# One 512-column pass for both parts of the operand, into two halves of a PSUM bank, with groups of two column tiles

## The chip, the cores and the metric

The kernel runs on one core of a Trainium2 chip. The metric is the device time of one execution in microseconds (us); lower is better. Engines are named as in the profile: PE is TensorE (matmul), PEld its weight load, DVE is VectorE, ACT ScalarE, POOL GpSimd, SP the sync engine, whose queue issues nearly all DMAs.

## The reference

Two layers act on a stream `h` of 256 positions by 4096 features; both also attend to a fixed memory of 256 tokens. All data are float32.

```
for i in range(2):
    proj = rmsnorm(h, pre_norm[i]) @ w_in[i]          # 4096 -> u 3072 | gate 3072 | q 1024 | q_gate 1024
    u, gate, q, q_gate = split(proj)
    y = s5_mixer(u) if i == 0 else rglru_mixer(u)
    kv = rmsnorm(mem, mem_norm[i]) @ w_kv[i]          # 4096 -> 2048
    m = 4-head softmax attention of q into kv
    out = concat([y * silu(gate), m * silu(q_gate)]) @ w_out[i]   # 4096 -> 4096
    h = h + rmsnorm(out, post_norm[i])
```

The S5 mixer is a complex diagonal state-space scan over the 256 positions (192 groups of 16 channels, 64 states each), then GELU and a gate by a product with a 3072 x 3072 matrix (`glu`). The RG-LRU mixer is a short convolution, two block-diagonal gates and a first-order recurrence.

## The kernel before, in words

**Products.** A float32 weight tile W and operand tile X are each split into a high and a low part of type float32r: `hi`, `lo` and `X[:, 0]`, `X[:, 1]`. Of the four products three are kept: `hi` by X high, `hi` by X low, `lo` by X high. Weights are the stationary side (128 x 128), the operand moves with its 256 positions, and the result is one column tile of 128 features by 256 positions in PSUM. In the V projections alone (`vproj`) the operand is stationary and 512 columns of weights move. The operand of a layer lies in SBUF as `[128, 2, 32, 256]`: part, row tile, position.

**The weight stream.** `add_phase` (L268) makes a list of 980 steps; each step takes one chunk of 512 KB, which is 8 weight tiles: usually 2 row tiles by 4 column tiles (`mc=4, kc=2`). A group of four column tiles needs 16 steps over 32 row tiles; it holds two PSUM banks, two column tiles in each. The phases in order are u0 (96 steps), g0 (96), gq0, q0, k0, v0, k1 (32 each), glu (72), out0 (128), v1 (32), u1 (96, with 12 gate steps of the RG-LRU between them and the phases after), gq1, q1 (32 each), g1 (96) and out1 (128). The first 8 tiles of u0 come in chunks of 8 x 1, the next 4 in chunks of 2 x 4.

**One turn.** `run` (L367) goes turn by turn, and what it emits is the program order of all engines. In a turn it first runs what is due (`at(k, f)` puts f into turn k) and the hooks of that step, then `mm_step(i)`, 24 matmuls, then `split_w(i + 2)`: two ScalarE casts of 512 columns to `hi`, and VectorE subtractions to `lo` that wait in a list `pieces`. Then comes `run_side`, the rest of the pieces, and `load_w`, the weight DMA some steps ahead (three buffers `raw`, six halves each of `hi` and `lo`). A turn in which `ready()` of the step is false runs all this without matmuls, and the step waits for the next turn.

**The side work** is generators (S5, attention, set-up of the RG-LRU). `run_side` (L356) takes the next piece of one only while the planner's running estimates allow it:

```
while self.side and self.dve_t < self.pe_t and self.act_t < self.pe_t:
```

The estimates are sums of prices in the code: a matmul of 256 columns 109, one of 512 columns 217, a VectorE tensor operation 1.04 per element and 70 more (`tt`, L74).

**S5** (L674). Its scan runs over 127 times t in two blocks of 48 state pairs. One t is a multiplication `m` (192 elements) and two additions (96 each); between them `seqfill` (L954) takes a waiting piece of the weight split or books 130, and small operations book 20 (`pen`) where no piece is there. In the scan a piece is 256 columns. After a block, `S = self.step + 6`, and `y_tasks(blk, ct, S + 5 * c // 2)` (L840) puts the output of each of 12 channel tiles into fixed turns: load of u at S, product `y_mm` at S + 2, activation steps at S + 3 to S + 8, stores of `gF` and `gHL` at S + 9. Coefficients are made on GpSimd (`y_coef`, L799). The second block's inputs are taken only as the first block's output products are done. `load_g` (L1233) brings the stored `gHL` into the operand buffer A in the turn after it is stored, and the GLU's step kg of the first group is ready once tiles 2 kg and 2 kg + 1 are asked for.

**Operands** are made by `prep_phase` (L252), 16 units of two row tiles, one per turn: two ScalarE and two VectorE operations each, and squares where a row scale is wanted. It starts at k0 - 14 for the memory of k0 and at k1 - 14 for k1, in the buffer A that the product before still reads.

**Evacuation.** When a group ends, its column tiles are evacuated one a turn from PSUM (`ev_*`, L401 to L557): a multiplication by the row scale, then what the phase needs. The output products (`whole`) take the two banks one after the other (`ev_out`, L452).

Of the kernel before, what the change touches and what calls it, by code (L numbers as in the profile page):

```python
# [20 lines left out]
T = 256  # L21
E = 3072
# [18 lines left out]

def size(ap):
    n = 1
    for s in ap.shape[1:]:
        n *= s
    return n


class Trunk:
# [185 lines left out]
    def prep(self, src, gain, layer, dst, ks, square=False, last=False, rb=None, col=None):  # L235
        """Operand tiles ks (a pair) of a normalised matrix: gain applied, split into two float32r parts."""
# [15 lines left out]
    def prep_phase(self, start, src, gain, layer, dst, square=False, rb=None, col=None, spacing=1):  # L252
        """16 units; the one for tiles 2c, 2c+1 runs at step start + c * spacing."""
        def load(c):
            if c >= KD // 2:
                return
            f = self.prep(src, gain, layer, dst(), (2 * c, 2 * c + 1), square, c == KD // 2 - 1, rb, col)

            def go():
                f()  # L260
                load(c + 2)
            self.hook(start + int(c * spacing), go)
        self.hook(start - 3, lambda: load(0))
        self.hook(start - 2, lambda: load(1))

# [1 line left out]
    def add_phase(self, w, nm, ks, operand, evac, mc=4, kc=2, vproj=False, ready=lambda kg: True, m0=0,  # L267
                  whole=False):  # L268
        """Matrix product with weight chunks of kc x mc tiles; ks: operand tiles in order of use."""
        nkg = len(ks) // kc  # L270
        for mg in range(nm // mc):
            grp = {}
            for kg in range(nkg):
                self.steps.append(dict(w=w, idx=mg * nkg + kg, mg=mg, kg=kg, nkg=nkg, grp=grp, mc=mc, kc=kc,
                                       ks=ks[kg * kc:kg * kc + kc], operand=operand, evac=evac, v=vproj, m0=m0, whole=whole,
                                       ready=(lambda mg=mg, kg=kg: mg > 0 or ready(kg))))
# [29 lines left out]
    def mm_step(self, i):  # L306
# [6 lines left out]
        grp, mc, kc = s["grp"], s["mc"], s["kc"]  # L313
        if s["kg"] == 0:
            if s["v"]:
                grp["acc"] = [self.ps_acc.tile([128, 512], F32, name="acc", tag="acc") for _ in range(2)]
            else:
# [3 lines left out]
        if end and not s["v"]:  # L321
            order = [(kk, (m,)) for m in range(mc) for kk in range(kc)]
        for kk, ms in order:
# [4 lines left out]
            if s["v"]:  # L328
                wh, wl = hi[kk], lo[kk]
                for n in range(2):  # L330
                    a = grp["acc"][n]
# [4 lines left out]
            else:  # L336
                for m in ms:
                    a = grp["acc"][m // 2][:, m % 2, :]
                    h, c = (kk * mc + m) // 4, (kk * mc + m) % 4 * 128
                    wh, wl = hi[h][:, c:c + 128], lo[h][:, c:c + 128]  # L340
# [3 lines left out]
        if s["kg"] == s["nkg"] - 1:  # L344
            acc = grp["acc"]
            if s["v"]:
                for n in range(2):
                    self.at(self.step + 1 + 2 * n, lambda n=n: s["evac"](s["m0"] + s["mg"], n, acc[n]))
            else:
                if s["whole"]:  # L350
                    self.at(self.step + 1, lambda: s["evac"](s["mg"] * mc, acc, 0))
                for m in range(0 if s["whole"] else mc):
                    self.at(self.step + 1 + (max(0, m - 1) if mc != 4 else m), lambda m=m: s["evac"](s["m0"] + s["mg"] * mc + m, acc[m // 2][:, m % 2, :]))
        del s["hi"], s["lo"]
# [12 lines left out]
    def run(self):  # L367
        """One turn per weight chunk; a turn without a chunk where its operand is not there yet."""
# [32 lines left out]
    def ev_u0(self, m, ps):  # L401
        """The even times first, then the odd ones."""
# [49 lines left out]
    def ev_out(self, layer, m, accs, i, out, last):  # L452
        """Tiles m, m + 1 of an output product: gain, sum of squares; then those of the next bank."""
# [6 lines left out]
        def b():  # L460
# [4 lines left out]
            if i == 0:  # L465
                self.ev_out(layer, m + 2, accs, 1, out, last)
# [17 lines left out]
    def boundary_begin(self):  # L484
        """h1 = x + out * rstd * gain, then the operand of layer 1; the first loads run ahead."""
# [106 lines left out]
    def exp_gen(self, y, x, t):  # L592
        """y = exp(x); t: list of 5 scratch tiles (the last one int32)."""
# [168 lines left out]
        # -- inputs of the odd states: B u[2t+1] + a B u[2t], two units of 32 channels in the rows --  # L762
# [21 lines left out]
        # -- outputs of the 128 channels ct --  # L784
# [140 lines left out]
    def s5_a_b(self, region, t0, n):  # L925
        """Stages that put a B of n channel tiles, with the channels in the rows, to memory."""
# [34 lines left out]
    def attention(self, layer, X):  # L961
# [21 lines left out]
        for h in range(4):  # L983
# [24 lines left out]
            pT = ap.tile([128, 2, T], F32, name="pT", tag="pT", bufs=1)  # L1008
# [25 lines left out]
    def lru_setup(self):  # L1034
# [8 lines left out]
        # log1p(z) = 2 atanh(z / (2 + z))  # L1043
# [20 lines left out]
    def lru_block(self, b, G):  # L1064
        """Conv, gates (their products in step G) and recurrence of the block's 256 channels."""
# [98 lines left out]
    def build(self):  # L1164
# [8 lines left out]
        allk = list(range(KD))  # L1173
# [4 lines left out]
        self.add_phase(I["w_u0a"], 8, allk, A, self.ev_u0, mc=8, kc=1)  # L1178
        self.add_phase(I["w_u0b"], 4, allk, A, self.ev_u0, mc=2, kc=4, m0=8)
        self.add_phase(I["w_u0c"], KE - 12, allk, A, self.ev_u0, m0=12)  # L1180
        self.add_phase(I["w_g0"], KE, allk, A, self.ev_silu(self.sil))
        self.add_phase(I["w_gq0"], KX, allk, A, self.ev_silu(self.sq[0]))
        self.add_phase(I["w_q0"], KX, allk, A, lambda m, ps: self.ev_row(self.qd[0], self.rbx)(m, ps))
        mark["k0"] = len(self.steps)
        self.add_phase(I["w_k0"], KX, allk, A, self.ev_row(self.kd[0], self.rbm))
        self.add_phase(I["w_v0"], KX, allk, A, self.ev_v(self.vd[0]), vproj=True)
        mark["k1"] = len(self.steps)
        self.add_phase(I["w_k1"], KX, allk, A, self.ev_row(self.kd[1], self.rbm))
        mark["glu"] = len(self.steps)

        self.add_phase(I["w_glu"], KE, list(range(KE)), A, self.ev_glu,
# [3 lines left out]
        self.add_phase(I["w_out0"], KD, list(range(KE, KD)) + list(range(KE)), B, self.ev_out0, whole=True,  # L1195
                       ready=lambda kg: ("att", 0) in self.done)
        mark["v1"] = len(self.steps)
        self.add_phase(I["w_v1"], KX, allk, A, self.ev_v(self.vd[1], "st"), vproj=True)
# [3 lines left out]
        def ev_u1(m, ps):  # L1202
            """One tile a turn, in order, once the row scale is there."""
# [9 lines left out]
        self.add_phase(I["w_u1"], KE, allk, B, ev_u1)  # L1213
        self.add_phase(I["w_gq1"], KX, allk, B, self.ev_silu(self.sq[1]))
        self.add_phase(I["w_q1"], KX, allk, B, lambda m, ps: self.ev_row(self.qd[1], self.rbx)(m, ps))
        mark["gate1"] = len(self.steps)
        self.add_phase(I["w_g1"], KE, allk, B, self.ev_g1)
# [6 lines left out]
        self.add_phase(I["w_out1"], KD, list(range(KE, KD)) + list(range(KE)), A, self.ev_out1, whole=True,  # L1224
                       ready=lambda kg: ("att", 1) in self.done)
# [21 lines left out]
        for k in range(KE):  # L1247
            self.hook(mark["glu"] - 16 + k // 2 + 2, lambda k=k: try_g(k))
# [22 lines left out]
        # the table of the square root is loaded ahead of the chain that needs it  # L1271
# [22 lines left out]
def layout(i):  # L1294
    """Host-side data layout only."""
# [3 lines left out]
    r["mem"] = np.ascontiguousarray(A["mem"][0].T).reshape(KD, 128, T)  # L1299
    for l in range(2):  # L1300
        w = A["w_in"][l]
        if l == 0:
            r["w_u0a"] = lay(w[:, :1024], 8, 1)
            r["w_u0b"] = lay(w[:, 1024:1536], 2, 4)
            r["w_u0c"] = lay(w[:, 1536:E])
        else:
            r["w_u1"] = lay(w[:, :E])
        r[f"w_g{l}"] = lay(w[:, E:2 * E])
        r[f"w_q{l}"] = lay(w[:, 2 * E:2 * E + XA])
        r[f"w_gq{l}"] = lay(w[:, 2 * E + XA:])  # L1310
        kv = A["w_kv"][l]
        r[f"w_k{l}"] = lay(kv[:, :XA])
        r[f"w_v{l}"] = lay(kv[:, XA:])
        o = A["w_out"][l]
        r[f"w_out{l}"] = lay(np.concatenate([o[E:], o[:E]], axis=0))
    r["w_glu"] = lay(A["s5_w_glu"][0])
# [51 lines left out]
```

## Time and profile before

| what | value |
|---|---|
| median of 3 runs | 3026.53 us (3025.53 to 3026.67) |
| span of the profiled execution, first to last instruction | 3025.3 us (its own time is not given apart) |
| PE busy | 2954.0 us, 98% |
| DVE busy | 2024.8 us, 67% |
| ACT busy | 1549.5 us, 51% |
| DMA | 645 MB, mean 213 GB/s |

The span leaves out what lies around the program. Busy times count a pipelined matmul from start to its modelled end, so overlapping passes are counted once as a union: a busy PE says that it always had a pass in flight, not how fast passes follow each other. That is read from the starts in a timeline, or from counts in a window (a count takes in passes that overlap an edge of it).

### The profile page before, as it was taken

To read this page: it belongs to the slowest core of one execution; us is meant where nothing else is said; L and a number is where in the kernel's file an instruction comes from. 1 tells how busy PE (TensorE), PEld (TensorE's weight loads), DVE (VectorE), ACT (ScalarE), POOL (GpSimd) and SP (SyncE) were. 2 spreads that over 40 slices of the span, in tenths; PEclk is the share of its full clock that TensorE was granted. 3 is DMA by queue.
4 is the path that set the end of the run, shared out by engine and by line. 5 is a ranking of instruction groups with operands and counts; after the bars stand their busy time and mean duration, and the time that the engine had idled before them with its cause. 6 is when DMAs were issued, how large, how long until landed. Compare 5 with 4: busy or idle time off the path is not lost.

```text
span 3025.3 us, 64511 instructions
## 1 busy us (share of the span) xinstructions
PE 2954.0 (98%) x24558; PEld 2901.3 (96%) x24558; DVE 2024.8 (67%) x4349; ACT 1549.5 (51%) x2871; POOL 164.0 (5%) x225
## 2 busy tenths in 40 slices
PE   9999999999999999999999998999999999999996
PEld 9999999999998988999999977999999999999996
DVE  8638998559999654656545565677787765645445
ACT  6444444554645644546544444456665655444443
POOL 1000000520000530000000011000000000000001
PEclk9999999999999999999999999999999999999998
DMA  8776656766767787567656588666666665556554
GB/s 266 224 211 213 210 192 204 231 218 201 240 207 229 252 267 241 197 218 241 211 192 198 190 254 238 199 198 216 193 223 205 209 222 184 189 200 197 196 190 159
DMA packets 286391, 644.87 MB, mean 213 GB/s; under 512 B 38912, under 2 KB 158976, under 8 KB 285824
## 3 DMA queue, kind: packets, MB, share of 16 engines
q1 hardware_dynamic: 279872, 634.72, 65.2%
q0 software_dynamic: 4352, 4.20, 0.9%
q8 instruction: 192, 3.15, 0.4%
q10 hardware_dynamic: 1856, 1.84, 0.2%
q14 instruction: 119, 0.97, 0.1%
HBM read 592.81 MB, written 47.81 MB: 212 GB/s over the span
## 4 chain that ended last, share of the span: by engine, by line
PE 89%; DMA 5%; DVE 2%; issue 1%; ACT 1%; SPq 1%; DVEq 0%; ACTq 0%; POOLq 0%
PE acc L116 85%; PE psx L116 1%; PE pm L116 1%; PE psg L116 1%; DMA bh<-in_x 1%; DVE lo L76 1%; SPq L120 1%; DMA u<-uF 1%; DMA st<-in_mem 1%; DMA bo<-og 0%; ACT hi L112 0%; DVE Bfin L76 0%; PE pso L116 0%; PE pss L116 0%; DMA gHL<-gh 0%
## 5 line engine op out<-in xcount | busy, mean ns | idle before, releaser
L76 DVE TENSOR_TENSOR lo<-raw,hi 128x512 fp32r<-128x512 f32 (+1 forms) x2386 | 1355.2, 598 | 864.5 <-ACT hi L112 806.6
L112 ACT CAST hi<-raw 128x512 fp32r<-128x512 f32 x1960 | 1165.1, 619 | 1013.1 <-PE acc L116 718.3
L116 PE MATMUL acc<-A,hi 128*128 128x256 f32 x8320 | 1513.0, 284 | 10.7 <-ACT A L108 6.3
L116 PEld LDWEIGHTS acc<-A,hi 128*128 128x128 f32 x8320 | 1299.7, 192 | 16.5 <-ACT A L108 6.3
L116 PE MATMUL acc<-A,lo 128*128 128x256 f32 x4160 | 1179.6, 284 | 2.3 <-DVE lo L76 2.2
L116 PEld LDWEIGHTS acc<-A,lo 128*128 128x128 f32 x4160 | 799.4, 192 | 4.6 <-DVE lo L76 4.5
L116 PE MATMUL acc<-Bhn,hi 128*128 128x256 f32 x4096 | 742.0, 284 | 7.2 <-ACT hi L112 7.2
L116 PEld LDWEIGHTS acc<-Bhn,hi 128*128 128x128 f32 x4096 | 640.4, 192 | 8.3 <-ACT hi L112 7.8
L116 PE MATMUL acc<-Bhn,lo 128*128 128x256 f32 x2048 | 580.4, 283 | 0.7 <-DVE lo L76 0.7
L116 PEld LDWEIGHTS acc<-Bhn,lo 128*128 128x128 f32 x2048 | 393.6, 192 | 1.3 <-DVE lo L76 1.3
L116 PE MATMUL acc<-Bmix,hi 128*128 128x256 f32 x2048 | 368.7, 283 | 0.0
L116 PEld LDWEIGHTS acc<-Bmix,hi 128*128 128x128 f32 x2048 | 319.5, 192 | 0.0
L116 PE MATMUL acc<-Bmix,lo 128*128 128x256 f32 x1024 | 289.8, 283 | 0.0
L116 PEld LDWEIGHTS acc<-Bmix,lo 128*128 128x128 f32 x1024 | 196.6, 192 | 0.0
L76 DVE TENSOR_TENSOR Bs<-Bs,m 128x96 f32<-128x96 f32 x508 | 169.0, 333 | 4.3
L116 PE MATMUL acc<-hi,A 128*128 128x512 f32 x512 | 160.7, 396 | 11.2 <-ACT hi L112 11.2
L116 PEld LDWEIGHTS acc<-hi,A 128*128 128x128 f32 x512 | 97.0, 191 | 32.9 <-ACT hi L112 12.9
L116 PE MATMUL acc<-lo,A 128*128 128x512 f32 x256 | 101.3, 396 | 0.0
L76 DVE TENSOR_TENSOR m<-A,Bs 128x192 f32<-128x192 f32 x254 | 90.6, 357 | 10.5 <-ACT Bs L112 4.4
L807 POOL TENSOR_TENSOR Bs<-Bs,cf 128x256 f32<-128x256 f32 x48 | 33.3, 693 | 784.6 <-DMA Bs<-in_s5c 418.7
L575 POOL TENSOR_TENSOR Bfin<-Bfin 128x1024 f32<-128x1024 f32 x4 | 10.3, 2586 | 1145.6 <-DVE Bfin L76 1145.6
L108 ACT ACTIVATE e<-e 128x256 f32<-128x256 f32 x64 | 26.8, 418 | 86.8 <-DVE e L76 86.4
(143 smaller groups left out, 1503.9 us busy)
## 6 DMA issues: line engine op xcount, KB each, us to landing
raw<-in_w_out SPq DMA_DIRECT2D x256, 512.0 KB, 3.9
raw<-in_w_g SPq DMA_DIRECT2D x192, 512.0 KB, 3.6
raw<-in_w_u SPq DMA_DIRECT2D x96, 512.0 KB, 3.9
raw<-in_w_glu SPq DMA_DIRECT2D x72, 512.0 KB, 3.8
raw<-in_w_gq SPq DMA_DIRECT2D x64, 512.0 KB, 4.2
raw<-in_w_q SPq DMA_DIRECT2D x64, 512.0 KB, 3.6
raw<-in_w_k SPq DMA_DIRECT2D x64, 512.0 KB, 4.0
raw<-in_w_v SPq DMA_DIRECT2D x64, 512.0 KB, 4.0
```

The source lines that it names most:

```text
L76: self.nc.vector.tensor_tensor(out=out, in0=a, in1=b, op=op)
L108: self.nc.scalar.activation(out=out, in_=a, func=f, **kw)
L112: self.nc.scalar.copy(out=out, in_=a)
L116: self.nc.tensor.matmul(out, lhsT=lhsT, rhs=rhs, start=start, stop=stop)
L120: self.nc.sync.dma_start(out=out, in_=in_)
L575: self.nc.gpsimd.tensor_tensor(out=o, in0=o, in1=h, op=ALU.add)
L807: g.tensor_tensor(out=P, in0=s["craw"], in1=b(re), op=ALU.mult)
```

## The change

Each group of column tiles gets a form: chunks of 8 x 1 (`n8`), 2 x 4 (`n2`), 4 x 2 (`n4`) column by row tiles as before, `v` for the V projections, and a new one, `w2`: 2 column by 4 row tiles. In `w2` each column tile has a bank of its own. One matmul of 512 columns multiplies `hi` by both parts of X, high part into the first half of the bank and low part into the second; one of 256 columns adds `lo` by X high to the second half. At evacuation ScalarE copies the second half into a new SBUF buffer `e0`, VectorE adds the first half, and the old evacuation goes on from SBUF.

Most phases are `w2` throughout. The first 12 tiles of u0, the first 4 of k0, k1 and glu, and the first 8 of u1 keep the old forms. The planner's prices in `w2` are 211 and 105 per pair of tiles. Some loads start later, because a group's last pass over the operand now takes 8 steps and not 16: the operand of k0 at k0 - 6, and the GLU's `gHL` at glu - 8 with four tiles a turn. To make room, `e3` has two buffers instead of three, and `pT` of the attention lies in `p`.

```diff
+SHAPE = {"n8": (8, 1), "n2": (2, 4), "n4": (4, 2), "w2": (2, 4), "v": (4, 2)}
+def blocks(nm, form=None, n=0):
+    return ([(0, n, form)] if form else []) + [(n, nm - n, "w2")]
+FORMS = {"u0": [(0, 8, "n8"), (8, 4, "n2"), (12, KE - 12, "w2")], "g0": blocks(KE), "gq0": blocks(KX), "q0": blocks(KX),
+         "k0": blocks(KX, "n4", 4), "v0": [(0, KX, "v")], "k1": blocks(KX, "n4", 4),
+         "glu": blocks(KE, "n4", 4), "out0": blocks(KD), "v1": [(0, KX, "v")],
+         "u1": blocks(KE, "n4", 8), "gq1": blocks(KX), "q1": blocks(KX), "g1": blocks(KE), "out1": blocks(KD)}
...
-                grp["acc"] = [self.ps_acc.tile([128, 2, T], F32, name="acc", tag="acc") for _ in range(mc // 2)]
+            n = 2 if form == "v" else mc if wide else mc // 2
+            grp["acc"] = [self.ps_acc.tile([128, 2, T], F32, name="acc", tag="acc") for _ in range(n)]
...
-                    a = grp["acc"][m // 2][:, m % 2, :]
+                if wide:
+                    a = acc[m]
+                    self.mm(a, wh, X[:, :, k, :], first, False, 211)
+                    self.mm(a[:, 1, :], wl, xh, False, last, 105)
+                else:
+                    a = acc[m // 2][:, m % 2, :]
                     self.mm(a, wh, xh, first and m % 2 == 0, False, 109)
                     self.mm(a, wh, xl, False, False, 109)
                     self.mm(a, wl, xh, False, last and m % 2 == 1, 109)
...
+    def evacuate(self, s, acc):
...
+        elif s["form"] == "w2":
+            t = self.ev.tile([128, 2, T], F32, name="e0", tag="e0", bufs=1)
+            for m in range(mc):
+                self.at(self.step + 1 + (0 if s["whole"] else 2 * m), lambda m=m: self.acopy(t[:, m, :], acc[m][:, 1, :]))
+            def add(m):
+                self.add(t[:, m, :], t[:, m, :], acc[m][:, 0, :])
+            def both():
+                add(0)
+                add(1)
+                evac(m0, [t], 0)
+            def one(m):
+                add(m)
+                evac(m0 + m, t[:, m, :])
+            if s["whole"]:
+                self.at(self.step + 2, both)
             else:
+                for m in range(mc):
+                    self.at(self.step + 2 + 2 * m, lambda m=m: one(m))
...
-            g, sg, o = self.e("e1"), self.e("e2"), self.e("e3")
+            g, sg = self.e("e1"), self.e("e2")
+            o = self.ev.tile([128, T], F32, name="e3", tag="e3", bufs=2)
...
-            if i == 0:
-                self.ev_out(layer, m + 2, accs, 1, out, last)
+            if i + 1 < len(accs):
+                self.ev_out(layer, m + 2, accs, i + 1, out, last)
...
-            pT = ap.tile([128, 2, T], F32, name="pT", tag="pT", bufs=1)
+            pT = p
...
-        self.prep_phase(mark["k0"] - 14, I["mem"], "memg", 0, A, True, self.rbm, self.colm)
+        self.prep_phase(mark["k0"] - 6, I["mem"], "memg", 0, A, True, self.rbm, self.colm)
...
-            self.hook(mark["glu"] - 16 + k // 2 + 2, lambda k=k: try_g(k))
+            self.hook(mark["glu"] - 8 + k // 4 + 2, lambda k=k: try_g(k))
```

The rest of the diff lays out the weight chunks by the same table and removes comments.

## Rows read from the trace of the kernel before

**Rows 1.** The page, part 1: engine, busy us, share, instructions.

```profile
PE 2954.0 (98%) x24558; PEld 2901.3 (96%) x24558; DVE 2024.8 (67%) x4349; ACT 1549.5 (51%) x2871; POOL 164.0 (5%) x225
```

**Rows 2.** Windows of PE on `acc`: stretch, length, busy, count, clock, DMA share, GB/s.

```profile
920.00:990.00 70.00, 70.00 (x311) 1.00 0.75 242
1500.00:1700.00 200.00, 200.00 (x1670) 1.00 0.60 196
```

**Rows 3.** Timeline of PE at 300 and 925 us: start, us, engine, line, operation.

```profile
300.18 0.28 PE L116 MATMUL acc<-A,lo 128*128 128x256 f32 x1
...
300.54 0.28 PE L116 MATMUL acc<-A,lo 128*128 128x256 f32 x1
...
924.92 0.39 PE L116 MATMUL acc<-lo,A 128*128 128x512 f32 x1
...
925.60 0.39 PE L116 MATMUL acc<-lo,A 128*128 128x512 f32 x1
```

**Rows 4.** Tile view of `m`: count, duration ns min/median/max, first and last start.

```profile
L76 DVE TENSOR_TENSOR m<-A,Bs x254: 342/358/372, 234.2 to 992.6; 128x192 f32<-128x192 f32 x127
```

**Rows 5.** Windows of all engines: PE, PEld, DVE, ACT, POOL, clock, DMA.

```profile
233.50:513.50 280.00, 280.00 (x2336) 280.00 (x2335) 261.69 (x823) 125.38 (x214) 0.00 (x0) 1.00 0.64 202
...
1004.00:1124.00 120.00, 110.60 (x1309) 105.94 (x1308) 68.36 (x112) 64.09 (x160) 62.45 (x96) 0.99 0.81 260
```

**Rows 6.** Chain that ended last, in order of time: start, us, what.

```profile
171.92 1.78 PE psx L116 x16
...
1095.68 1.60 PE pm L116 x50
...
1100.81 3.67 DMA u<-uF
...
1150.77 4.74 DMA gHL<-gh
```

**Rows 7.** Groups of instructions, passes with `lo`: busy us, mean ns, idle before.

```profile
L116 PE MATMUL acc<-A,lo 128*128 128x256 f32 x4160 | 1179.6, 284 | 2.3 <-DVE lo L76 2.2
...
L116 PE MATMUL acc<-Bhn,lo 128*128 128x256 f32 x2048 | 580.4, 283 | 0.7 <-DVE lo L76 0.7
...
L116 PE MATMUL acc<-Bmix,lo 128*128 128x256 f32 x1024 | 289.8, 283 | 0.0
```

**Rows 8.** Groups: a VectorE read of 256 PSUM columns, a ScalarE copy of them.

```profile
L76 DVE TENSOR_TENSOR e<-acc,rbx 128x256 f32<-128x256 f32 x128 | 52.9, 415 | 26.3 <-DMA uF<-e 18.5 <-DMA qd<-e 5.4 <-PE acc L116 2.3
...
L112 ACT COPY Bs<-psa 128x256 f32<-128x256 f32 x1 | 0.4, 374 | 2.6 <-PE psa L747 2.6
```

**Rows 9.** Windows of PE on `acc`, each from the start of the span.

```profile
0.00:538.00 538.00, 507.33 (x4160) 1.00 0.70 218
...
0.00:1124.20 1124.20, 1050.80 (x8272) 1.00 0.71 224
...
0.00:233.50 233.50, 204.69 (x1642) 1.00 0.76 235
...
0.00:660.00 660.00, 613.11 (x5021) 1.00 0.70 220
```

**Rows 10.** Tile views of `psx` and `pm`: passes that read a buffer named `acc`.

```profile
L116 PE MATMUL psx<-acc,W x192: 270/275/275, 542.4 to 660.2; 128*128 128x128 f32 x192
...
L116 PE MATMUL pm<-ones,acc x40: 164/250/271, 75.8 to 3000.9; 128*128 128x1 f32 x40
```

**Rows 11.** Tile views of `Bs`, `gHL` and `u`: GpSimd coefficients, SP issues, DMA landing.

```profile
L807 POOL TENSOR_TENSOR Bs<-Bs,cf x48: 612/616/1089, 523.9 to 1107.3; 128x256 f32<-128x256 f32 x48
...
L809 POOL TENSOR_TENSOR Bs<-Bs,cQ x48: 455/514/967, 525.7 to 1108.6; 128x128 f32<-128x128 f32 x48
...
L120 SPq DMA_DIRECT2D A<-gHL x48: 319/407/1241, 1064.0 to 1156.3; - x48
...
DMA to landing us min/median/max: 3.2/3.8/5.8
```

More of the change, by code (lines that the diff above doesn't have):

```diff
@@ L264, in prep_phase, with add_phase @@
         self.hook(start - 2, lambda: load(1))
[L267 to L276, printed above, removed]
+    def add_phase(self, name, operand, evac, ks=None, whole=False, ready=lambda kg: True):
+        idx = 0
+        first = True
+        w = self.I["w_" + name]
+        for m0, nm, form in FORMS[name]:
+            mc, kc = SHAPE[form]
+            kk = ks or list(range(KD))
+            nkg = len(kk) // kc
+            for mg in range(nm // mc):
+                grp = {}
+                for kg in range(nkg):
+                    self.steps.append(dict(w=w, idx=idx, m=m0 + mg * mc, kg=kg, nkg=nkg, grp=grp, mc=mc, kc=kc,
+                                           ks=kk[kg * kc:kg * kc + kc], operand=operand, evac=evac, form=form,
+                                           whole=whole,
+                                           ready=(lambda kg=kg: ready(kg)) if first else (lambda: True)))
+                    idx += 1
+                first = False
     def load_w(self, i):
@@ L312, in mm_step @@
         X = s["operand"]()
-        grp, mc, kc = s["grp"], s["mc"], s["kc"]
+        grp, mc, kc, form = s["grp"], s["mc"], s["kc"], s["form"]
+        wide = form == "w2"
         if s["kg"] == 0:
-            if s["v"]:
-                grp["acc"] = [self.ps_acc.tile([128, 512], F32, name="acc", tag="acc") for _ in range(2)]
-            else:
-                grp["acc"] = [self.ps_acc.tile([128, 2, T], F32, name="acc", tag="acc") for _ in range(mc // 2)]
+            n = 2 if form == "v" else mc if wide else mc // 2
+            grp["acc"] = [self.ps_acc.tile([128, 2, T], F32, name="acc", tag="acc") for _ in range(n)]
+        acc = grp["acc"]
         end = s["kg"] == s["nkg"] - 1
         order = [(kk, range(mc)) for kk in range(kc)]
-        if end and not s["v"]:
+        if end and form != "v":
             order = [(kk, (m,)) for m in range(mc) for kk in range(kc)]
@@ L327, in mm_step @@
             xh, xl = X[:, 0, k, :], X[:, 1, k, :]
-            if s["v"]:
+            if form == "v":
                 wh, wl = hi[kk], lo[kk]
                 for n in range(2):
-                    a = grp["acc"][n]
+                    a = acc[n].rearrange("p a b -> p (a b)")
                     r = slice(n * 128, n * 128 + 128)
@@ L343, in mm_step @@
                     self.mm(a, wl, xh, False, last and m % 2 == 1, 109)
[L344 to L348, printed above, removed]
-            else:
[L350 to L354, printed above, removed]
+        if end:
+            self.evacuate(s, acc)
+        del s["hi"], s["lo"]
+    def evacuate(self, s, acc):
+        m0, mc, evac = s["m"], s["mc"], s["evac"]
+        if s["form"] == "v":
+            for n in range(2):
+                self.at(self.step + 1 + 2 * n, lambda n=n: evac(m0 // 4, n, acc[n].rearrange("p a b -> p (a b)")))
+        elif s["form"] == "w2":
[13 more added lines that the diff above has]
+                self.at(self.step + 2, both)
+            else:
+                for m in range(mc):
+                    self.at(self.step + 2 + 2 * m, lambda m=m: one(m))
+        elif s["whole"]:
+            self.at(self.step + 1, lambda: evac(m0, acc, 0))
+        else:
+            for m in range(mc):
+                self.at(self.step + 1 + (max(0, m - 1) if mc != 4 else m),
+                        lambda m=m: evac(m0 + m, acc[m // 2][:, m % 2, :]))
     def run_side(self):
@@ L1172, in build @@
         self.A = self.big.tile([128, 2, KD, T], F32R, name="A", tag="A")
-        allk = list(range(KD))
         A, B = (lambda: self.A), (lambda: self.B)
@@ L1176, in build @@
         mark = {}
[L1178 to L1183, printed above, removed]
+        self.add_phase("u0", A, self.ev_u0)
+        self.add_phase("g0", A, self.ev_silu(self.sil))
+        self.add_phase("gq0", A, self.ev_silu(self.sq[0]))
+        self.add_phase("q0", A, lambda m, ps: self.ev_row(self.qd[0], self.rbx)(m, ps))
         mark["k0"] = len(self.steps)
[L1185 to L1186 removed]
+        self.add_phase("k0", A, self.ev_row(self.kd[0], self.rbm))
+        self.add_phase("v0", A, self.ev_v(self.vd[0]))
         mark["k1"] = len(self.steps)
[L1188 removed]
+        self.add_phase("k1", A, self.ev_row(self.kd[1], self.rbm))
         mark["glu"] = len(self.steps)
[L1191 removed]
+        self.add_phase("glu", A, self.ev_glu, ks=list(range(KE)),
                        ready=lambda kg: ("gload", 2 * kg + 1) in self.done)
         mark["out0"] = len(self.steps)
[L1195 removed]
+        self.add_phase("out0", B, self.ev_out0, ks=list(range(KE, KD)) + list(range(KE)), whole=True,
                        ready=lambda kg: ("att", 0) in self.done)
         mark["v1"] = len(self.steps)
[L1198 removed]
+        self.add_phase("v1", A, self.ev_v(self.vd[1], "st"))
         mark["u1"] = len(self.steps)
@@ L1299, in layout @@
     r["mem"] = np.ascontiguousarray(A["mem"][0].T).reshape(KD, 128, T)
+    W = {"glu": A["s5_w_glu"][0]}
     for l in range(2):
[L1301 to L1316, printed above, removed]
+        w, kv, o = A["w_in"][l], A["w_kv"][l], A["w_out"][l]
+        W[f"u{l}"], W[f"g{l}"] = w[:, :E], w[:, E:2 * E]
+        W[f"q{l}"], W[f"gq{l}"] = w[:, 2 * E:2 * E + XA], w[:, 2 * E + XA:]
+        W[f"k{l}"], W[f"v{l}"] = kv[:, :XA], kv[:, XA:]
+        W[f"out{l}"] = np.concatenate([o[E:], o[:E]], axis=0)
+    for n, w in W.items():
+        r["w_" + n] = np.concatenate([lay(w[:, m * 128:(m + c) * 128], *SHAPE[f]) for m, c, f in FORMS[n]])
     ga = np.stack([A["lru_w_a"][0], A["lru_w_x"][0]], axis=1)
```

18 lines of the change are left out of this document (9 added, 9 removed).

## The prediction

> **What bounds the kernel now.** I read the page's engine shares first: TensorE is busy 98% of the span, VectorE 67% [rows 1]. The busy share alone says little of a pipelined engine, so next came stretches counted by matmul. In 200 us of plain weight products TensorE starts or ends 1670 passes of 256 columns; in a stretch of the V projection, 311 passes of 512 columns in 70 us, both at a granted clock of 1.00 [rows 2]. The timeline gives the period free of edge effects: passes with `lo` start at 300.18 and 300.54 us, 0.36 us for three 256-column passes, so 120 ns each; in the V projection at 924.92 and 925.60 us, 0.68 us for three, so 226.7 ns each [rows 3]. Every one of these passes has its own weight load. So the period is not proportional to columns: two narrow passes cost 240.0 ns, one of double width 226.7, and each pass carries a fixed 2 × 120.0 − 226.7 = 13.3 ns. In the plain stretches no engine but TensorE sets the pace.
>
> The second bound is a chain through VectorE. The S5 scan runs from 234.2 us to 992.6 [rows 4], and in its first half VectorE is busy 262 of 280 us [rows 5]. Its results are the operand of the GLU product, and the chain that ended last passes through them: the store of `gHL` at 1150.77 us lies on it [rows 6].
>
> **The wide pass.** The `lo` passes number 4160 + 2048 + 1024 = 7232 [rows 7], so that many (column tile, row tile) pairs have three narrow passes. The new table of forms leaves 12 tiles × 32 of u0, 4 × 32 each of k0 and k1, 4 × 24 of the GLU and 8 × 32 of u1 as they were: 992. The other 6240 get one wide and one narrow pass: 226.7 + 120.0 = 346.7 ns for 360.0. That is 6240 × 13.3 = 83 us, the main term. Eight pairs make a step, before and after: a step falls from 2.880 to 2.773 us, on 780 of 980 steps. The trace shows no wide pass whose moving operand lies in two pieces (`hi` and `lo` parts of X), nor a narrow one behind a wide one. Bounds of the pair: above, 360.0, where the wide pass costs two narrow ones; below, the narrow pass falls to the least period that a pass with its own 128 × 128 load shows here, 1.78 us for 16 or 111 ns [rows 6], 9 ns and 56 us more. I take 346.7, from the rows with the same columns, type and loads.
>
> The Trainium skill ("TensorE: Matmul & The Clock Gate", section "Back-to-back issue gap") puts a warm pass at N/2.4 + 2.5 ns, a fixed part of 2.5. By that rule the saving would be 6240 × 2.5 = 16 us, an estimate from that page. This trace disagrees: 120.0 and 226.7 ns [rows 3] where the page's formula has 109.2 and 215.8.
>
> **Evacuation and the moved steps.** 200 tiles (12 + 24 + 8 + 8 + 4 + 4 + 20 + 32 + 16 + 8 + 8 + 24 + 32) each add a ScalarE copy, 0.374 us, and a VectorE add, 0.415 us by the nearest rows [rows 8]: 75 and 83 us in all, 0.09 and 0.10 us per step. Outside the scan the idle third of VectorE hides it. The banks don't bind: a group of two tiles holds two of four for 8 steps, and they are read by the fourth turn after, four turns before they are wanted. It is exposed at two places, after the last matmul and at the end of out0: two copies and two adds, 1.6 us, where some 0.2 us of the second bank's round go; about 1.4 us each, 3 us. `pT` in `p`, two buffers for `e3` and one `e0` cost nothing, since each is free again within the 8 turns between groups. The operand loads of k0 (from k0 − 6, not k0 − 14) keep 6 turns, 17 us, ahead of their use, over transfers that land in about 4 us. Four GLU tiles a turn, not two, put 8 issues of 0.41 us [rows 11] into SP's queue ahead of that turn's weights: 0 to 5 us; I take 0, as three chunks are in flight.
>
> **The S5 scan becomes late.** `run_side` issues a scan step only while the planner's VectorE estimate is under its TensorE estimate, so the program order follows these estimates, not the chip. A turn is worth 24 × 109 = 2616 before and 8 × (211 + 105) = 2528 now, and each tile adds 336 to VectorE, 84 per turn.
> Where events lie in turns, from the passes on `acc` counted up to a time [rows 9], less 8 per norm sum and 192 that read inputs of the scan from a buffer of that name [rows 10]: block 0 starts at turn (1642 − 8)/24 = 68; the first S5 output product is at (4160 − 8)/24 = 173, 8 after the scan's end (`S` = end + 6, product at `S` + 2), so the end is 165; block 1 starts at (5021 − 200)/24 = 201; the last output product stands at 8272 − 208 = 8064 passes, 288 × 24 + 384 + 32 × 24, so at turn 352 = `S` + 29: `S` = 323, end 317. `g` of tile 23 is stored at `S` + 36 and loaded in turn 360; the GLU (steps from 352, two tiles a step) wants it at 363. Slack: 3 turns.
> The budget of a turn: four pieces of the weight split, 4 × 336 = 1345; a scan step 270 + 2 × 170 = 610 and up to 430 for unfilled slots, of which pieces fill about 300 a turn. Block 0, before: 97 × 2616 = 254k offered; 97 × (1345 − 300) + 127 × 1040 + 14k of evacuations + 6k of side work = 253k. It closes. After: 2528 − 1045 − 252 (168 in u0) leaves 1231 a turn for 132 + 6 − 2k: 110 turns, 13 more. Block 1 starts at 214, not 201 (between the blocks `y_tasks` counts the turns). Before, it had 116 turns, 303k against 296k by the same sum; I carry the 7.6k. After, by turn 320 it has 10 × 1231 + 32 × 1315 + 16 × 1487 + 16 × 1315 + 32 × 1559 = 149k, less 24k and 11k for the two operand phases and the 7.6k: 107k of 132k. The other 25k take 18 turns of k1: end at 338, 21 later. With 3 of slack, some 18 turns of the GLU's first group find no operand and run without a chunk.
> What they cost: from turn 359 to 381 (five of the group's steps, 5 turns for each two tiles) TensorE has 4.5 steps, 13 us, and six output products of 1.6 us [rows 6], 10 us. A turn there is bounded by GpSimd, 4 × 0.62 + 4 × 0.5, some 4.5 us a tile or 1.8 a turn, and by the round of u load (3.8 us to land), product, VectorE, store, spread over several turns [rows 11]. I take 2.0 us: 44 − 23 = 21 us without work, less about 5 of the 9 us that TensorE idles now from 1004 to 1124 us [rows 5], since half of these tiles no longer interleave there: 16 us. Ends: 1.5 us a turn gives +5, one landing of 4 us per turn +60.
> In the scan itself VectorE would need 0.935 × 2.880 × 2528/2616 = 2.60 us of a 2.773 us turn: covered, barely.
>
> **Sum.** The profiled span is 3025.3 us; the shown runs have a median of 3026.53, and I carry the 1.2 us over. 3026.5 − 83 + 3 + 16 = 2962 us.
>
> **Rivals.** *The scan costs nothing* (short late turns, or pieces that fill more slots): 3026.5 − 83 + 3 = 2946. For it, the S5 tail needs few us of any engine; against it, the 3 turns of slack. *VectorE binds in the scan*: its 94% becomes the pace, the 226 turns of both blocks stay at 2.880 us, 24 us are lost: 2986. *A landing for each late turn*: 3026.5 − 83 + 3 + 60 = 3006; for it, a u load of 3.67 us stands on the chain at 1100.81 us [rows 6]. *No change*: most of the fixed part belongs to loads and columns, and 2 to 4 ns go per pair; 6240 × 3.0 = 19 us pays for the late scan and the tails and no more: 3027. Against it, the two periods of rows 3. The 2.5 ns of the Trainium skill's page "TensorE: Matmul & The Clock Gate" would put the time at about that value. *Slower*: the moving operand lies in two pieces 32 KB apart and the wide pass costs two narrow ones; nothing is saved, the 19 us of late scan and tails stay: 3045. It decides from 240.0 − 3.0 = 237.0 ns on. Against it, the V projection's 226.7, though with an operand in one piece.
>
> **Chances.** Forecast 0.50, scan free 0.17, VectorE bound 0.08, long late turns 0.13, no change 0.05, slower 0.07. A difference under 0.2% (6 us) can't be told from none here: faster 0.88, same 0.05, slower 0.07. The range goes some way under the free scan, for a cheaper narrow pass, and to just past the long turns: 2928 to 3008.
>
> **What would show it.** Right: in plain stretches passes with `lo` start 0.347 us apart; the scan's last `m` lies beyond turn 330 by count; TensorE has gaps at the GLU's first group, with `gHL` just before; the first 48 steps are unchanged. Wrong: a period of 0.36 us (no change or slower), waits for `lo` all through 250 to 500 us (VectorE bound), or a first GLU group without gaps.

## The result and the profile after

The changed kernel is slower: 3042.1 us (3037.6 to 3056.5, five runs) against 3025.5 us before (3016.4 to 3026.7), a ratio of 1.0065 with a 95% interval of 1.004 to 1.0089. The forecast was 2962 us, the range 2928 to 3008; the time lies outside of it, on the other side of no change. (The median of the kernel before moved between 3026 and 3035 us from one set of runs to the next, so experiments below are told as ratios to the kernel before of the same set. A difference between two such ratios, as between an experiment and the changed kernel, is uncertain by some 0.3%, or 9 us; stages come from one profile each.)

The page of the changed kernel: engine, busy us, share, instructions; then two rows of its 40 slices.

```profile
PE 2923.2 (96%) x18318; PEld 2582.6 (85%) x18318; DVE 2084.3 (69%) x4597; ACT 1586.9 (52%) x3073; POOL 165.4 (5%) x225
...
PE   9999999999999977999999998999999999999996
...
PEclk9999999999999987999999999999999999999998
```

6240 passes and weight loads are gone, and TensorE's share fell from 98 to 96%: it now waits, above all in slices 15 and 16 (1064 to 1216 us), where its clock dips too.

The wide pass itself costs what was forecast. In the timeline of TensorE in out1 (start, us, operation) 17 pairs take 2765.68 − 2759.79 = 5.89 us, 346.5 ns a pair; before, a pair took 360 [rows 3].

```profile
2759.79 0.27 PE L130 MATMUL acc<-A,lo 128*128 128x256 f32 x1
2760.13 0.28 PE L130 MATMUL acc<-A,lo 128*128 128x256 f32 x1
...
2765.68 0.28 PE L130 MATMUL acc<-A,lo 128*128 128x256 f32 x1
```

The time went in three places. Here is the program by stages, each taken from the first weight issue of its first phase on SP's queue to that of the next (us):

| stage | before | after | forecast of the change | change |
|---|---|---|---|---|
| start to the GLU's weights | 1107.9 | 1083.5 | −26 for wide passes, and some of the S5 tail moves behind it | −24 |
| GLU | 236.9 | 304.6 | −6, and that tail with its late turns | +68 |
| out0 | 368.1 | 356.5 | −14 | −12 |
| v1, u1, gq1, q1 | 607.3 | 600.4 | −14 | −7 |
| g1 | 296.7 | 302.4 | −10 | +6 |
| out1 and the end | 408.4 | 393.0 | −14 + 1 | −15 |

The stages ahead of the GLU are 24 us shorter, but only because output work of the scan moved into the GLU's stage: at the first weights of out0 the changed kernel is 43 us behind. Of the stages from there on, only out0 and out1 give what was forecast. Rows for the two boundaries of the GLU: tile views of the weights of the GLU and of out0 and out1 together (issue time in ns min/median/max, first and last start in us), the kernel before, then the changed kernel.

```profile
L120 SPq DMA_DIRECT2D raw<-in_w_glu x72: 327/332/535, 1107.9 to 1342.2; - x72
...
L120 SPq DMA_DIRECT2D raw<-in_w_out x256: 327/328/436, 1344.8 to 2982.6; - x128
```

```profile
L134 SPq DMA_DIRECT2D raw<-in_w_glu x72: 327/333/661, 1083.5 to 1385.3; - x72
...
L134 SPq DMA_DIRECT2D raw<-in_w_out x256: 327/328/448, 1388.1 to 2998.0; - x128
```

**The late scan.** Tile views of `m` and `pm` and windows of TensorE on `acc` from the start (length, busy, count, clock), the changed kernel; the answers to rows 4, 9 and 10:

```profile
L90 DVE TENSOR_TENSOR m<-A,Bs x254: 340/358/371, 231.8 to 1056.6; 128x192 f32<-128x192 f32 x127
```

```profile
L130 PE MATMUL pm<-u,d x48: 270/275/552, 572.8 to 1180.0; 128*128 128x128 f32 x48
```

```profile
0.00:572.80 572.80, 538.87 (x3384) 1.00 0.72 218
0.00:699.40 699.40, 644.18 (x4025) 1.00 0.72 219
0.00:1058.40 1058.40, 1002.44 (x6193) 1.00 0.72 220
```

With 24 passes in an old step and 16 in a wide one, the first S5 product stands at turn 187 (forecast 186), block 1 starts at 215 (forecast 214) and the scan ends at about 342 (forecast 338). The planner's sum was right. In us the scan ended at 1058 instead of 994. TensorE then met the GLU's first group without its operand. Timeline of TensorE, with what ended each idle time:

```profile
1085.09 0.77 PE L130 MATMUL pm<-u,d 128*128 128x128 f32 x2 [6.37 <-DMA u<-uF]
...
1127.05 1.11 PE L130 MATMUL acc<-A,hi 128*128 128x256 f32 x2 [5.05 <-DMA A<-gHL]
...
1142.44 0.94 PE L130 MATMUL acc<-A,hi 128*128 128x256 f32 x2 [1.20 <-DMA A<-gHL]
```

The gap at 1127.05 is the GLU's seventh step, which waits for tile 13. SP's timeline has the loads of tiles 13, 15 and 23, which `y_tasks` and `load_g` put into turns `S` + 12, `S` + 17 and `S` + 37:

```profile
1125.01 0.79 SPq L134 DMA_DIRECT2D A<-gHL  x2
...
1140.29 0.79 SPq L134 DMA_DIRECT2D A<-gHL  x2
...
1194.54 0.80 SPq L134 DMA_DIRECT2D A<-gHL  x2
```

That is 25 turns in 69.5 us, 2.8 us a turn, and 15 us for the first five; the forecast took 22 turns of 2.0. On the chain there ScalarE's next `gh` waits until the store of the last one has landed (it has one buffer), and the load into A until its own store has. Landings of `gHL` and A make up 29 of the 69.5 us, TensorE's passes 23, and ScalarE, VectorE and SP the rest. Chain of the changed kernel, start, us, what:

```profile
1134.15 1.77 DMA gHL<-gh
1136.00 0.41 ACT gh L126
...
1138.25 2.03 DMA gHL<-gh
1140.29 2.11 DMA A<-gHL
1142.44 3.08 PE acc L130 x12
1145.52 2.18 PE pm L130 x47
```

The passes there are slow as well. In the timeline nine passes take 1.92 us, 213 ns each where 120 is usual [rows 3], and the window of TensorE shows a granted clock of 0.50, the lower of its two levels (1.2 of 2.4 GHz):

```profile
1143.18 0.41 PE L130 MATMUL acc<-A,lo 128*128 128x256 f32 x1
...
1145.10 0.41 PE L130 MATMUL acc<-A,lo 128*128 128x256 f32 x1
```

```profile
1142.40:1145.60 3.20, 3.16 (x14) 0.50 0.73 231
```

Windows of all engines (PE, PEld, DVE, ACT, POOL, clock, DMA):

```profile
1100.00:1150.00 50.00, 38.90 (x463) 35.76 (x466) 23.89 (x42) 23.16 (x63) 25.22 (x41) 0.83 0.61 192
1150.00:1200.00 50.00, 31.99 (x309) 26.77 (x302) 17.53 (x32) 16.90 (x48) 16.04 (x26) 0.64 0.56 174
```

**Loads of the GLU's evacuation.** This was not in the forecast. Who waited for whom from 1200 to 1420 us, us in total, times, longest:

```profile
ACT Bmix L126 <- DVE e L90: 74.7, 23, 4.8
DVE lo L90 <- ACT hi L126: 48.5, 44, 8.4
DVE e L90 <- DMA st<-gF: 47.7, 23, 5.6
```

The kernel before, in the same work without its first group (1190 to 1360 us):

```profile
DVE e L76 <- DMA st<-gF: 6.1, 8, 2.2
```

VectorE waits for `gF` 23 times, two us each, where it waited 8 times under one. The evacuation of a tile issues its load into `st` and multiplies by it in the next turn. SP issues the load in line behind the weights, and the landing, 4.96 us in the instance below, falls on VectorE. SP's timeline:

```profile
1342.25 4.27 SPq L134 DMA_DIRECT2D raw<-in_w_glu  x3
...
1346.57 0.43 SPq L134 DMA_DIRECT2D st<-gF  x1
```

Before, four tiles followed in four turns and two `st` buffers let landings overlap, with eight turns to recover. Now the tiles come two turns apart and each pays alone. Behind the waiting multiplication stand the next `lo`, and the ScalarE copy to `Bmix` with the next `hi` behind it, so TensorE waits. One instance on the chain:

```profile
1346.57 4.96 DMA st<-gF
...
1352.78 0.62 ACT hi L126
...
1353.43 0.70 DVE lo L90
...
1354.17 5.70 PE acc L130 x31
```

### The profile page after: what moved, and what is told of

Read it like the earlier page. It is cut to its first block, busy times and chain, and to the rows that moved or that the text cites. A ratio compares the mean times of both kernels' runs of the same rounds, so it can differ in the third digit from the quotient of the medians.

```text
span 3040.4 us, 52558 instructions
## 1 busy us (share of the span) xinstructions
PE 2923.2 (96%) x18318; PEld 2582.6 (85%) x18318; DVE 2084.3 (69%) x4597; ACT 1586.9 (52%) x3073; POOL 165.4 (5%) x225
## 4 chain that ended last, share of the span: by engine, by line
PE 80%; DMA 8%; DVE 6%; issue 2%; ACT 2%; SPq 1%; ACTq 0%; DVEq 0%; POOLq 0%
PE acc L130 76%; DVE lo L90 3%; DMA st<-gF 1%; PE pm L130 1%; DMA gHL<-gh 1%; PE psg L130 1%; PE psx L130 1%; ACT hi L126 1%; SPq L134 1%; DMA bh<-in_x 1%; DVE e L90 1%; DMA u<-uF 1%; DVE Bs L90 1%; DMA bo<-og 1%; DVE Bfin L90 0%
## 5 line engine op out<-in xcount | busy, mean ns | idle before, releaser
L90 DVE TENSOR_TENSOR lo<-raw,hi 128x512 fp32r<-128x512 f32 (+1 forms) x2434 | 1341.2, 587 | 773.3 <-ACT hi L126 734.5
L126 ACT CAST hi<-raw 128x512 fp32r<-128x512 f32 x1960 | 1139.9, 618 | 771.7 <-PE acc L130 358.4
L130 PE MATMUL acc<-A,hi 128*128 128x512 f32 (+1 forms) x4896 | 1494.6, 367 | 37.5 <-DMA A<-gHL 21.5
L130 PEld LDWEIGHTS acc<-A,hi 128*128 128x128 f32 x4896 | 886.1, 192 | 196.3 <-DMA A<-gHL 20.8
L130 PE MATMUL acc<-Bhn,hi 128*128 128x512 f32 (+1 forms) x2304 | 726.4, 373 | 13.2 <-ACT hi L126 13.2
L130 PEld LDWEIGHTS acc<-Bhn,hi 128*128 128x128 f32 x2304 | 419.7, 190 | 92.4 <-ACT hi L126 15.4
L130 PE MATMUL acc<-Bmix,hi 128*128 128x512 f32 x1024 | 355.6, 391 | 0.4 <-ACT hi L126 0.4
L130 PEld LDWEIGHTS acc<-Bmix,hi 128*128 128x128 f32 x1024 | 191.5, 187 | 42.9 <-ACT hi L126 0.7
L126 ACT COPY e<-acc 128x256 f32<-128x256 f32 x200 | 73.5, 368 | 75.6 <-PE acc L130 74.7
L90 DVE TENSOR_TENSOR e<-e,acc 128x256 f32<-128x256 f32 x200 | 79.5, 410 | 7.1 <-ACT e L126 7.1
```

The costliest lines, as they stand in the source:

```text
L90: self.nc.vector.tensor_tensor(out=out, in0=a, in1=b, op=op)
L126: self.nc.scalar.copy(out=out, in_=a)
L130: self.nc.tensor.matmul(out, lhsT=lhsT, rhs=rhs, start=start, stop=stop)
```

## The experiments

My theory after the result: the lost gain lies (1) in the late scan and (2) in the single-tile loads of the GLU and of g1, which has the same pattern with `hs`. The rival to (1) was that VectorE itself is the limit in the scan, whatever the planner counts; the rival to (2) that the copies and adds of the new evacuation chain the engines and the loads only happen to end last.

**e1, the planner's prices.**

```diff
-                    self.mm(a, wh, X[:, :, k, :], first, False, 211)
-                    self.mm(a[:, 1, :], wl, xh, False, last, 105)
+                    self.mm(a, wh, X[:, :, k, :], first, False, 218)
+                    self.mm(a[:, 1, :], wl, xh, False, last, 109)
```

> The changed kernel with the planner's prices of a pair set to 218 and 109 (2616 a turn, as before) and nothing else. Theory (the scan is issued too slowly because a turn is worth less to the planner): block 1 of the scan ends some 10 turns earlier, the GLU's first group has some 13 late turns where the changed kernel has about 23, at about 3.3 us each: 3010 us. Rival (VectorE itself is the limit in the scan): the scan's turns only get longer, waits for lo appear between 250 and 1050 us, 3035 to 3045 us.

Ratio 1.0028 (1.0011 to 1.0045): a third of the forecast gain, 0.37% or 11 us. By the same count as above the scan ends at turn 332, ten earlier as expected, though still 15 later than before. The GLU's stage shortened by 21 us (283), but the GLU began 13 us later (1096.9): the scan's turns grew. Both theories hold in part.

**e2, early loads.** One turn after a wide group ends, both tiles' loads are issued.

```diff
         elif s["form"] == "w2":
+            src = {self.ev_glu: (self.gF, self.sil), self.ev_g1: (self.hs,)}.get(evac) if not s["whole"] else None
+            if src:
+                self.at(self.step + 1, lambda: [self.pre_st(m0 + m, src) for m in range(mc)])
...
     def ev_glu(self, m, ps):
-        st = self.stp.tile([128, 2, T], F32, name="st", tag="st")
-        self.dma(st[:, 0, :], self.gF[m])
-        self.dma(st[:, 1, :], self.sil[m])
+        if m not in self.pre:
+            self.pre_st(m, (self.gF, self.sil))
+        st = self.pre.pop(m)
...
```

`pre_st` takes a buffer `st` and issues its loads; `ev_g1` is changed like `ev_glu`.

> The changed kernel, but in the wide groups of the GLU and of g1 the loads into st for both tiles are issued one turn after the group ends, with the copy of the first tile, and not with each tile's evacuation. Theory (each tile now pays a DMA landing of its own on VectorE, which four tiles in four turns shared before): waits of VectorE on st fall from 48 to under 15 us in the GLU, 25 us there and 10 in g1 come back: 3005 us. Rival (ScalarE and VectorE are chained by the copy and the add, the loads only happen to end last): under 8 us, 3035 to 3042 us.

Ratio 0.9971 (0.9957 to 0.9986): 0.94% or 28 us under the changed kernel, where 35 were expected. The waits of VectorE on `gF` fell from 47.7 us to this (1160 to 1420 us of e2):

```profile
DVE e L91 <- DMA st<-gF: 7.0, 4, 4.3
```

The loads were the cause; the copies and adds stayed and did no such harm. Read from the stages the gain is 18 us: the GLU takes 293 us for 305 and g1 296 for 302. Two more pairs that differ in this edit alone say 21 (e4 against e1) and 22 (e7 against e3), so 28 is its upper side.

**e3, old forms up to the GLU.** In `FORMS` u0, g0, gq0, q0, k0 and k1 get `n8`, `n2` and `n4` throughout, and the two load hooks go back to k0 − 14 and glu − 16 + k // 2 + 2.

```diff
-FORMS = {"u0": [(0, 8, "n8"), (8, 4, "n2"), (12, KE - 12, "w2")], "g0": blocks(KE), "gq0": blocks(KX), "q0": blocks(KX),
-         "k0": blocks(KX, "n4", 4), "v0": [(0, KX, "v")], "k1": blocks(KX, "n4", 4),
+FORMS = {"u0": [(0, 8, "n8"), (8, 4, "n2"), (12, KE - 12, "n4")], "g0": [(0, KE, "n4")], "gq0": [(0, KX, "n4")],
+         "q0": [(0, KX, "n4")], "k0": [(0, KX, "n4")], "v0": [(0, KX, "v")], "k1": [(0, KX, "n4")],
```

> The changed kernel with the old forms and the old places of the operand loads in all phases up to k1; GLU and everything behind it as changed. Theory (the late scan costs the pre-GLU gain and more): the scan ends in time, no gap at the GLU's first group, 17 + 58 us less the 25 that the wide passes gave before the GLU: about 3000 us. Rival (the GLU's gap comes from its own wide groups and the four loads a turn, not from the scan): the GLU stage stays 60 us longer than before, 3045 us or more.

Ratio 0.9963 (0.9946 to 0.9979), 31 us under the changed kernel, where some 40 were expected. The scan ended at 999 us again and the GLU's stage took 246 us for 305. So the wide form ahead of the GLU, with its groups of two and its price in the planner, did not merely fail to pay, it cost the kernel 1%.

**e4, e1 and e2 together.**

> The two edits of e1 and e2 together. If both theories hold and act in different stretches the gains add: about 2975 us. If only the prices count 3010, if only the loads count 3005, if neither 3040.

Ratio 0.9932 (0.9905 to 0.9959): 1.33% under the changed kernel, near the sum of 0.37 and 0.94. Within an uncertainty of 0.4% the two gains add; the 2975 us were missed because the size of the first was wrong.

**e5, the price alone.** The kernel before, with `109` replaced by `2528 / 24` in its six 256-column calls.

```diff
-                    self.mm(a, wh, xh, first and m % 2 == 0, False, 109)
+                    self.mm(a, wh, xh, first and m % 2 == 0, False, 2528 / 24)
```

> The kernel before with one edit: the planner's price of a 256-column pass is 105.3, so a turn is worth 2528 as in the changed kernel; no wide pass, no copies and adds. Theory (the price alone delays the scan): the scan ends some 14 turns later, about 11 late turns at the GLU's first group, some 3 us each: 20 to 35 us slower, 3045 to 3060 us. Rival (VectorE's added work delays it, the price does not matter): unchanged, 3025 us.

Ratio 1.0099 (1.0076 to 1.0122), 30 us slower. Nothing on any engine was added; a number in the planner delayed the scan to 1061 us, turn 340 by count, 23 later than before where 14 were expected, and the GLU's stage took 293 us for 237. The operations of the scan that VectorE started or ended from 235 to 505 us (window, busy, count) show the pace, first in the kernel before, then the changed kernel, then e5:

```profile
235.00:505.00 270.00, 126.43 (x371) 1.00 0.64 203
```

```profile
235.00:505.00 270.00, 109.57 (x324) 1.00 0.67 202
```

```profile
235.00:505.00 270.00, 110.37 (x324) 1.00 0.61 200
```

324 for 371 in both: 13% fewer in the same time.

**e6, three narrow passes in the new structure.**

```diff
-                    self.mm(a, wh, X[:, :, k, :], first, False, 211)
+                    self.mm(a[:, 0, :], wh, xh, first, False, 106)
+                    self.mm(a[:, 1, :], wh, xl, False, False, 105)
```

> The changed kernel with the wide pass replaced by two passes of 256 columns into the two halves of the bank, with the same total price; groups, copies, adds and loads as changed. Theory (the wide pass saves 13.3 ns for each of 6240 pairs wherever TensorE sets the pace, not in the GLU's stage and little in the scan): 55 to 80 us slower than the changed kernel, 3095 to 3120 us. Rival (other engines set the pace by now and the wide pass is worth nothing): 3040 to 3055 us.

Ratio 1.0183 (1.0168 to 1.0198): the wide pass is worth 1.2%, 36 us in this kernel, between the two forecasts. It also prices the rest of the change: without the wide pass the new structure is 1.83%, 55 us, slower than the kernel before. By the two profiles 39 of 42 us lie behind the first weights of out0 (1691.7 us to the end against 1652.3). Up to there the two kernels are 3 us apart (1391.2 and 1388.1), with or without 300 steps of wide passes. So what the wide passes gain ahead of out0 is lost again ahead of out0. Windows of TensorE on `acc` in the scan, the changed kernel and e6:

```profile
300.00:400.00 100.00, 100.00 (x579) 1.00 0.69 205
400.00:550.00 150.00, 149.26 (x831) 1.00 0.66 196
```

```profile
300.00:400.00 100.00, 100.00 (x836) 1.00 0.63 203
400.00:550.00 150.00, 150.00 (x1253) 1.00 0.63 198
```

From 300 to 400 us the changed kernel starts or ends 579 passes, the wide rate. From 400 us on it has 831 in 150, so 16 passes, a turn, take 2.89 us; in e6 a turn is 24 passes and takes 150 × 24 / 1253 = 2.87. In that stretch the wide passes are waited away. What waits are the weight loads, which need `hi` and `lo`. The changed kernel's waits from 400 to 550 us, and its engines (PE, PEld, DVE, ACT, POOL) in the first 50 us of that:

```profile
PEld acc L130 <- ACT hi L126: 3.5, 9, 0.7
PEld acc L130 <- DVE lo L90: 3.0, 11, 0.3
```

```profile
400.00:450.00 50.00, 49.75 (x276) 41.74 (x275) 45.04 (x143) 20.77 (x42) 0.00 (x0) 1.00 0.64 195
```

The 6.5 us of waits over 52 turns are 0.125 us a turn, as much as lies between 2.773 and 2.89. VectorE is busy 90% there, 2.60 us a turn. In the kernel before and in e6 TensorE's weight loads show no wait for `hi` or `lo` from 235 to 530 us.

**e7 and e9, e2 and e3 together** (the same kernel, run in two sets).

> Old forms and old load places up to k1 (as e3) and the early st loads (as e2). Theory (the changed kernel loses its gain to the late scan before the GLU and to the single-tile loads in the GLU and g1, and to nothing else): 1.5% under the kernel before, 2980 us where that takes 3025. If the two overlap or something else is lost too: 3005 to 3015.

> The kernel of e7 again, beside e8 on the same chip: 0.989 of the kernel before, as in e7.

Ratios 0.989 (0.9872 to 0.9908) and 0.9879 (0.9862 to 0.9896): 1.1 to 1.2% faster than the kernel before, 2996 and 2997 us. This is the best version found. It lacks 0.3 to 0.4% of my sum; u1, gq1 and g1, where the RG-LRU blocks load VectorE, still take 297, 102 and 296 us for 299, 99 and 297 before, though their 192 wide steps have 20 us less TensorE work. In e7 weight loads wait 9.5 us for `hi` and `lo` from 2110 to 2600 us, with VectorE busy 69 to 81%; in the kernel before none waits there.

**e8, higher prices and early loads.** As e4, with 225 and 113.

> The changed kernel with early st loads (as e2) and the planner's prices of a pair at 225 and 113, 2704 a turn, which pays for the added copies and adds, so that the scan needs as many turns as before and no turn is late. If the planner's count is all that delays the scan, the wide pass now gains before the GLU too: 0.981 to 0.984 of the kernel before. If VectorE's own time paces the scan (its share was 93% there in both kernels), turns of the scan stay at 2.88 us or more, the GLU starts no earlier than before, and the time is that of e7, 0.988 to 0.993.

Ratio 0.9902 (0.9885 to 0.9918). With 2704 a turn the scan keeps the pace of before (355 operations in 235 to 505 us for 371), and the phase g0 then takes 304 us, as long as before (302), though its TensorE work is 10 us shorter. So it is not the planner's count alone, and the wide pass gains nothing beside the scan. Window of all engines in e8, 235 to 530 us:

```profile
235.00:530.00 295.00, 291.27 (x1632) 248.87 (x1631) 275.17 (x864) 128.93 (x247) 0.00 (x0) 1.00 0.68 200
```

VectorE is busy 93%, as before [rows 5]; 295 × 16 / 1632 = 2.89 us a turn. Weight loads wait 8.2 us for `hi` and 5.1 for `lo`; `hi` waits 78 us for weights to land, and SP's queue, which issues them, waits 213 us for `lo`. That is a round: VectorE's `lo` frees one of three `raw` buffers, SP loads it, ScalarE makes `hi`, VectorE the next `lo`. VectorE has by far the most work in it, but waits 14 us for `hi` itself. Whether its time or the three buffers bind is not shown; no run had a fourth buffer.

**e10, TensorE kept busy in late turns.** The added passes' result is unused.

```diff
                 self.pe_t += 2616
+                d = self.ps_x.tile([128, 2, T], F32, name="pdum", tag="x")
+                for _ in range(6):
+                    self.mm(d[:, 0, 0:128], self.ident, self.ones, True, True, 0)
```

> The changed kernel with six matmuls of 128 columns into a scratch bank in each turn without a chunk (about 1.3 us of TensorE), so that TensorE does not fall idle among the late turns. Their result is not used. If the halved clock there (granted 0.64 in 1150 to 1200 us) is what makes a late turn 3.3 us: the clock stays near 1, the GLU's stage shortens by 10 to 15 us, about 3028 us. If the round of DMA landings sets the late turns: the stage keeps its 305 us or grows by the added passes, 3040 to 3060 us.

Ratio 1.0052 (1.0034 to 1.0069), not told apart from the changed kernel's 1.0065. Windows of all engines in e10:

```profile
1100.00:1150.00 50.00, 44.43 (x563) 41.52 (x562) 22.75 (x40) 23.09 (x69) 26.90 (x45) 0.93 0.67 207
1150.00:1200.00 50.00, 42.06 (x436) 38.82 (x436) 16.25 (x31) 16.27 (x43) 10.77 (x19) 0.90 0.54 165
```

The clock rose from 0.64 to 0.90 and the GLU's stage stayed at 303 us (305). The tile view of the added passes:

```profile
L130 PE MATMUL pdum<-ones,ident x240: 273/275/583, 1130.2 to 1190.3; 128*128 128x128 f32 x120
```

There are 20 late turns (the profile counts 12 passes for the six), and the passes of one take some 1.4 us by the starts in a timeline (24 of them from 1143.15 to 1145.93 us): 28 us of TensorE work in all. So filling the gaps does not pay, but e10 does not show that the lower clock costs nothing, since the added passes stand ahead of the useful ones and can eat what the higher clock gives. The landings stay the largest part of the chain; that they set the length of a late turn is argued, not shown. A second buffer for `gh` would test it.

## Why the prediction was wrong

- *The wide pass, "6240 × 13.3 = 83 us, the main term".* The price was right (346.5 ns a pair), its worth was not: 36 us by e6. The step that failed is the multiplication by all 6240 pairs. 2400 of them (300 steps) lie ahead of out0, where e6 shows 3 us for them. Counted behind it, 480 steps × 0.107 = 51 us were forecast and 39 measured. (The lower bound of the pair used 111 ns for a pass of 128 columns, from a piece of the chain; by the starts 16 of them take 1.70 us, 106 ns. The forecast did not rest on it. The formula with 2.5 ns that the prediction quotes from the Trainium skill ("TensorE: Matmul & The Clock Gate", section "Back-to-back issue gap") is given there for a single isolated pass, not for passes that each load their weights. The pair's 346.5 ns sides with the rows.)
- *The structure, "+ 3 + 16".* By e6 it costs 55 us without the wide pass, 36 more than the 19 of the sum. With the 47 us that the wide pass fell short this is the miss of 80, within the noise. The next points say where the 36 lie.
- *"In the scan itself VectorE would need ... 2.60 us of a 2.773 us turn: covered, barely."* The 2.60 us were right (90% of 2.89 us), "covered" failed: from 400 to 550 us the weight loads waited for `hi` and `lo`, and a turn took 2.89 us. What I left out is the order in line: `lo` stands behind the scan's operations on VectorE, and the next weights behind `lo`. I had given this a rival of its own (24 us, chance 0.08), and that was too little.
- *The S5 scan becomes late.* Right, and by nearly the right count (342 for 338). The price alone is enough for it (e5: turn 340), and with the price mended the added copies and adds still leave 15 turns (e1). *"I take 2.0 us"* a late turn failed: 2.8 us measured, 69.5 us for 25 turns where 44 for 22 were forecast. I weighed GpSimd's throughput, and on the chain stand landings (29 us) and passes at the lower clock (23 us).
- *"Outside the scan the idle third of VectorE hides"* the new evacuation. This failed for the GLU and g1, not by the 83 us of adds but by the spacing of tiles: 18 to 28 us by e2. I had counted what the new instructions cost and not what the new order does to instructions that stayed.
- The tails, the PSUM banks, the moved operand loads and the smaller buffers did what was forecast so far as the stages can show it: out0 and out1 gained 12 and 15 us.
- *The slower rival* came true in its sign but not in its mechanism: the wide pass with an operand in two pieces is no dearer. The rivals were each worked out singly; the time came from two of them at once (long late turns, a scan that VectorE's work does not cover) and a cause that was missing, the spaced loads.

Left open: the 0.3 to 0.4% that e7 lacks of its sum. By its rows it lies in u1, gq1 and g1, where the waits of the weight loads (9.5 us) are about half of the 20 us that did not come; no run took the RG-LRU's load off VectorE there.

## What to carry to other kernels

A pass saved is worth its price only where TensorE sets the pace, so sort the steps by stage before multiplying. A busy share under 100% does not say that an engine's work is covered: here weight loads waited with VectorE at 90% in the scan and at 69 to 81% in layer 1. Ask what stands in line ahead of each operation that another engine needs. When a planner's price sets the program order, changing that price is an edit of its own: test it alone. When work is regrouped, follow the loads that wait one turn for their landing: bunched, they share it, spaced out, each pays.

## What the runs showed of the hardware

- Passes of float32r operands, each with its own weight load, follow at 120.0 ns with 256 columns and at 226.7 with 512, at a granted clock of 1.00. If every column costs the same, 13.3 ns of a pass are fixed. A moving operand in two pieces 32 KB apart costs nothing more: 346.5 ns for the pair, 226.7 + 120.0 from the stretches before.
- Among gaps of 1 to 6 us TensorE's granted clock fell to a mean of 0.64 over 50 us; where it was 0.50, passes of 256 columns followed at 213 ns for 120. Six small matmuls in each late turn held the mean at 0.90 and changed nothing in the time, at 1.4 us of TensorE for each turn.
